# One inverse instead of two through DRAM, and memory attention in a written order, in a float32 two-block model

## The chip, the cores and the metric

The kernel runs on one core of a Trainium2 chip. What counts is the device time of one execution in microseconds (us). The engines of the core work side by side, each through its own list of instructions in order: TensorE (PE, with its weight loads as PEld), VectorE (DVE), ScalarE (ACT), GpSimd (POOL) and SyncE (SP), whose queue issues the loads of the weights. Semaphores tie the lists together. TensorE's clock has two levels, 1.2 and 2.4 GHz; the profile gives the granted clock as a share of the higher one.

## The reference

Two models stand one behind the other on one sequence of 256 tokens of width 1024, all in float32. The first has two layers of a mixer (three kinds of attention), a cross attention to 256 memory tokens, and an MLP, each with a layer norm behind it. The cross attention is:

```python
def memory_cross_attention(x, mem, w_q, w_kv, w_o):
    q = (x @ w_q).reshape(B, S, XA_HEADS, DH)                 # 4 heads of 64
    kv = (mem @ w_kv).reshape(B, M, 2, XA_HEADS, DH)
    k, v = kv[:, :, 0], kv[:, :, 1]
    s = jnp.einsum('bqhd,bmhd->bhqm', q, k) * (DH ** -0.5)
    p = jax.nn.softmax(s, axis=-1)
    o = jnp.einsum('bhqm,bmhd->bqhd', p, v).reshape(B, S, XA_W)
    return o @ w_o
x = layer_norm(DN_ALPHA * x + y, ln_g[l, 1], ln_b[l, 1])      # behind it
```

The second has two layers with three branches (a pooling mixer, retention, and an RWKV-7 recurrence), gated and merged. The recurrence goes token by token:

```python
def step(S, inp):
    r_t, w_t, k_t, v_t, a_t, b_t = inp
    sa = jnp.einsum('bhvk,bhk->bhv', S, a_t)
    S = S * w_t[:, :, None, :] + sa[..., None] * b_t[:, :, None, :] + v_t[..., None] * k_t[:, :, None, :]
    return S, jnp.einsum('bhvk,bhk->bhv', S, r_t)
```

## The kernel before

**Products.** Each float32 operand is split into a high part (`hi`, rounded) and the rest (`lo`), and a product is three matmuls, hi·hi, hi·lo and lo·hi (lines L138 to L140). Weights stream: SyncE's queue loads tiles of 512 KB into four buffers named `raw`, ScalarE casts `hi` (L112), VectorE, or GpSimd where a call says so, subtracts `lo` (L113); `hi` and `lo` have six buffers each. A matmul needs both, and a buffer `raw` comes free when its `lo` is done.

**Order.** A scheduler sets each engine's order from the order of the code and its own estimates of durations. Inside `tc.manual_schedule` TensorE's order is that of the code. PSUM banks are handed out by tag: four "mm", two "s", one "t", one "o". Copies out of PSUM by `evac` alternate between ScalarE (L283) and VectorE (L285).

**The recurrence in chunks.** Chunks of 64 tokens need the inverse of a triangular 64x64 matrix for each of eight heads and both halves of the partitions. The kernel writes the matrices to DRAM (`lt`), reads them back as 16x16 diagonal blocks, one to a partition, and inverts these by back substitution on VectorE (up to L1107) in `zrow`. It then copies `zrow` with rows and columns exchanged into `tb` (L1108), and GpSimd's queue writes both to scratch in DRAM: `td` from `tb` (L1111) and `zd` from `zrow` (L1112), each 128 KB. `inverse_parts` (L1116) reads them back as block diagonal tiles, `Tn` from `td` and `TT`, the transposed one, from `zd`, with eight reads of 128 KB (L1122). `invert` doubles the block size twice, with products of 64x64 matmuls (L1130), 16 instructions for one n of two. Meanwhile come retention's projections (`rv` evacuated by VectorE at L1322), its scores (L1334, L1339 on TensorE, masked by VectorE at L1336 and L1342), a gate (evacuated at L1292) and retention's outputs (L1351, L1354).

**How the recurrence is interleaved.** `recurrence` is a generator with 17 steps. `other_branches` is a second one with 16 yields, between which stand chunks of 12 matmuls of 512 columns or 24 of 256. In a `manual_schedule` the code takes one step of the one, then one of the other, and at last what is left of the others. At the recurrence's end VectorE normalises the outputs of each head (`ymu` L1250, `yvr` L1256, GpSimd's power at L174, L1258) and TensorE transposes them (`normed`, L1265).

**Memory attention** (block 1, once in each layer) lies between two norms. `us_k` and `us` are the weights of the keys and the query, split on GpSimd. `query` is 48 matmuls of 256 columns, `memory_values` 48, 24 for each half t of the tokens; `memory_scores` (L263) and the softmax (L266, L274), `memory_weights` (normalise L292, transpose L295), `attend_memory` (L307, with four casts and four subtractions of 128 columns), the output product with 12 matmuls of 512 columns for each t and c, and the second norm (`finish`: L338 and L340 on VectorE, transposes L343). Their order on TensorE is the scheduler's.

```python
        memory_keys(us_k)
        query(us)
        ps_ = [memory_scores(0)]
        memory_values()
        ps_.append(memory_scores(1))
```

Of the kernel before, what the change touches and what calls it, by code (L numbers as in the profile page):

```python
# [12 lines left out]
F32 = mybir.dt.float32  # L13
# [4 lines left out]
ALU = mybir.AluOpType  # L18
# [24 lines left out]
def program(ctx: ExitStack, tc: tile.TileContext, T: dict, out: bass.AP):  # L43
# [268 lines left out]
    class Norm:  # L312
# [17 lines left out]

        def finish(self, t):
            mv = st("mv", [128, 2])
            ver.bn_aggr(out=mv, in_=self.stats[t])
            r = rsqrt(mv[:, 1:2], LN_EPS)
            for i in range(2):
# [3 lines left out]
                                         op0=ALU.subtract, op1=ALU.mult)  # L339
                ver.scalar_tensor_tensor(out=z, in0=z, scalar=r, in1=self.b[:, s], op0=ALU.mult, op1=ALU.add)  # L340
                p = pst("s" if self.op else ("s", "s", "t", "o")[2 * t + i])
                for k in range(4):
# [37 lines left out]
    def block1_layer(l, x, xop, us, K):  # L380
# [352 lines left out]

        def memory_values():
            us = [unit(T["xa_kv"][l, 2 + i], 256, 4) for i in range(2)]
            o = [pst("mm"), pst("mm")]
            gemm_a(o, memop, us, n=256)
            for t in range(2):
                act.copy(out=xakv[:, 1, t], in_=o[t][:, :256])

# [6 lines left out]
        def memory_scores(t):  # L747
            return scores(256, lambda i: (xq[64 * (i // 2):64 * (i // 2) + 64, i % 2, tok(t)],
                                          xakv[64 * (i // 2):64 * (i // 2) + 64, 0, i % 2, :]), None)

        def memory_weights(P, sums):
            sc = st("sc", [128, 4])
            ver.reciprocal(out=sc, in_=sums)
            return transposed(P, sc, 256, ("s", "t"))

        def attend_memory(t, pt):
            for pr in range(2):
                pv_pair(xo, pr, t, lambda half: [(xakv[:, 1, kt, 128 * pr + 64 * half:128 * pr + 64 * half + 64],
                                                  pt[kt][:, pr + 2 * half, :]) for kt in range(2)])

# [17 lines left out]
        memory_keys(us_k)  # L778
        query(us)
        ps_ = [memory_scores(0)]  # L780
        memory_values()
        ps_.append(memory_scores(1))
        us = [unit(T["xa_o"][l, i], 512, 2) for i in range(2)]
        nrm2 = Norm(x)
        nrm2.params(l, 1)
        ahead = [unit(T["w_up"][l, i], 512, 2) for i in range(4)]
        ps_ = [memory_weights(*p) for p in ps_]
        for t in range(2):
            attend_memory(t, ps_[t])
            for c in range(2):  # L790
                o = [None, None]
                o[t] = pst("mm")
                gemm_a(o, xo, us[c:c + 1])
                nrm2.add(t, c, o[t])
            nrm2.finish(t)
        xop = nrm2.op
# [107 lines left out]
    def block2_layer(l, x, r, us, K, xop):  # L904
# [196 lines left out]
        for i in range(14, -1, -1):  # L1101
# [23 lines left out]
        def invert(Tn):  # L1125

# [142 lines left out]

        def recurrence(Tn):  # L1270

            yield from invert(Tn)
# [50 lines left out]

        Tn = inverse_parts()
        oop = Op([None, None, None])
# [231 lines left out]

    scratch = {n: dr.tile([128 * 2080], F32, name=n) for n in ("zd", "td", "lt")}

# [248 lines left out]
```

## Time and profile before

| | |
|---|---|
| median of 3 runs | 1672.89 us (1668.97 to 1673.03) |
| profiled execution, its own time | 1675.49 us |
| span in the trace | 1673.6 us |
| mean granted clock of TensorE | 0.973 |
| TensorE busy | 1588.1 us, 95% |
| VectorE, ScalarE, GpSimd busy | 1104.7, 742.7, 280.1 us |
| moved from and to HBM | 282.52 MB read, 6.88 MB written |

Block 1 ends at about 965 us of the span, block 2 fills the rest. A row of waits names the waiting engine and line, what released it, the sum in us, how often, and the longest. A row of a line of time gives start, duration, engine, line, operation, tiles and shape, and in brackets the idle time before and what ended it.

### The profile page before, as it was taken

Reading aid. Unit: us, or ns where it says so; the run is one execution under the profiler, and the core shown is the slowest. Engines: PE = TensorE matmul, PEld = TensorE weight load, DVE = VectorE, ACT = ScalarE, POOL = GpSimd, SP = SyncE. Lnnn points to the kernel's source line nnn. Section 1 sums busy time; section 2 is a strip of 40 time slices with the busy share of each in tenths; the row PEclk is TensorE's granted clock in tenths of the full one; section 3 lists DMA queues with packets and bytes.
Section 4 is the critical chain, followed back from the end, with each engine's and each line's share of the span. In section 5 each row is a group of like instructions: output and inputs, shape, how many; then the busy total and the mean of one; then the engine's idle time right before and its main releaser. Section 6 shows DMA issues by size and latency. Waiting matters only on the chain. (4 is left out here: it accounts for less than half of the span.)

```text
span 1673.6 us, 29627 instructions
## 1 busy us (share of the span) xinstructions
PE 1588.1 (95%) x11978; PEld 1442.6 (86%) x11978; DVE 1104.7 (66%) x1801; ACT 742.7 (44%) x1212; POOL 280.1 (17%) x266
## 2 busy tenths in 40 slices
PE   7999998999999999998999989889999999699998
PEld 6787997798878888986989879879999889699997
DVE  5557567876776665678966677665556677555654
ACT  4655444454445654444544364323443643233441
POOL 1000112111100000231201132401111313201202
PEclk9899999999999999999999979989999989899999
DMA  8732466487776333663777835643355345533552
GB/s 295 265 127 76 139 206 209 139 282 263 266 252 208 101 102 102 199 204 124 252 247 264 280 105 170 160 129 114 113 187 180 102 139 167 152 105 112 175 179 74
DMA packets 81752, 291.34 MB, mean 174 GB/s; under 512 B 9400, under 2 KB 10496, under 8 KB 81616
## 3 DMA queue, kind: packets, MB, share of 16 engines
q1 hardware_dynamic: 78768, 280.07, 50.8%
q0 software_dynamic: 2848, 9.39, 2.2%
q8 instruction: 94, 1.54, 0.4%
q14 instruction: 42, 0.34, 0.1%
HBM read 282.52 MB, written 6.88 MB: 173 GB/s over the span
## 5 line engine op out<-in xcount | busy, mean ns | idle before, releaser
L113 DVE TENSOR_TENSOR lo<-raw,hi 128x1024 fp32r<-128x1024 f32 (+1 forms) x421 | 532.8, 1272 | 282.1 <-ACT hi L112 280.5
L112 ACT CAST hi<-raw 128x1024 fp32r<-128x1024 f32 (+1 forms) x435 | 452.7, 1048 | 581.5 <-PE mm L139 242.6
L138 PE MATMUL mm<-act,hi 128*128 128x256 f32 x1808 | 523.3, 290 | 2.0 <-DVE act L130 2.0
L139 PE MATMUL mm<-act,hi 128*128 128x256 f32 x1808 | 520.0, 288 | 0.0
L140 PE MATMUL mm<-act,lo 128*128 128x256 f32 x1808 | 518.9, 287 | 0.0
L138 PEld LDWEIGHTS mm<-act,hi 128*128 128x128 f32 x1808 | 351.4, 194 | 7.2 <-issue 2.7
L139 PEld LDWEIGHTS mm<-act,hi 128*128 128x128 f32 x1808 | 351.0, 194 | 4.7 <-issue 4.3
L140 PEld LDWEIGHTS mm<-act,lo 128*128 128x128 f32 x1808 | 350.7, 194 | 2.6 <-issue 2.3
L138 PE MATMUL s<-act,hi 128*128 128x256 f32 x448 | 128.2, 286 | 6.9 <-ACT PT L834 4.3
L138 PE MATMUL mm<-hi,act 128*128 128x512 f32 (+1 forms) x320 | 125.1, 392 | 5.5 <-ACT hi L127 4.9
L140 PE MATMUL s<-act,lo 128*128 128x256 f32 x448 | 127.6, 285 | 0.0
L139 PE MATMUL s<-act,hi 128*128 128x256 f32 x448 | 127.6, 285 | 0.0
L139 PE MATMUL mm<-lo,act 128*128 128x512 f32 (+1 forms) x320 | 123.6, 386 | 0.8 <-DVE lo L113 0.8
L140 PE MATMUL mm<-hi,act 128*128 128x512 f32 (+1 forms) x320 | 123.2, 385 | 0.0
L138 PEld LDWEIGHTS s<-act,hi 128*128 128x128 f32 x448 | 86.8, 194 | 8.3 <-ACT PT L834 4.9
L139 PEld LDWEIGHTS s<-act,hi 128*128 128x128 f32 x448 | 86.7, 194 | 0.2
L140 PEld LDWEIGHTS s<-act,lo 128*128 128x128 f32 x448 | 86.8, 194 | 0.0
L839 POOL TENSOR_TENSOR PT<-PT 128x512 f32<-128x512 f32 x28 | 38.6, 1378 | 241.2 <-ACT P L838 115.1
L138 PEld LDWEIGHTS mm<-hi,act 128*128 128x128 f32 x320 | 60.9, 190 | 19.5 <-ACT hi L127 4.9
L1545 DVE CUSTOM_DVE_ANT_0 raw<-raw,gt 128x1024 f32<-128x1024 f32 x48 | 59.9, 1250 | 26.0 <-DMA raw<-in_w_ada 25.9
L138 PE MATMUL mm<-hi,P 128*128 128x512 f32 x192 | 74.8, 390 | 0.0
L139 PE MATMUL mm<-lo,P 128*128 128x512 f32 x192 | 74.8, 390 | 0.0
(486 smaller groups left out, 2418.2 us busy)
## 6 DMA issues: line engine op xcount, KB each, us to landing
raw<-in_w_in SPq DMA_DIRECT2D x119, 512.0 KB, 4.8
raw<-in_w_up SPq DMA_DIRECT2D x64, 512.0 KB, 4.7
raw<-in_w_down SPq DMA_DIRECT2D x64, 512.0 KB, 4.7
raw<-in_w_gate SPq DMA_DIRECT2D x48, 512.0 KB, 3.3
raw<-in_w_ada SPq DMA_DIRECT2D x48, 512.0 KB, 4.7
raw<-in_w_gl SPq DMA_DIRECT2D x48, 512.0 KB, 3.5
raw<-in_w_branch SPq DMA_DIRECT2D x24, 512.0 KB, 3.4
raw<-in_w_br SPq DMA_DIRECT2D x16, 512.0 KB, 3.3
```

The costliest lines, as they stand in the source:

```text
L112: act.copy(out=h[:, :cols], in_=r[:, :cols])
L113: (eng or ver).tensor_sub(out=l[:, :cols], in0=r[:, :cols], in1=h.bitcast(F32)[:, :cols])
L138: pe.matmul(o, lhsT=lh, rhs=rh, start=first, stop=False)
L139: pe.matmul(o, lhsT=lh, rhs=rl, start=False, stop=False)
L140: pe.matmul(o, lhsT=ll, rhs=rh, start=False, stop=last)
L839: pool.tensor_mul(out=r, in0=r, in1=r)
L1545: ver.tensor_tensor_reduce(out=r, in0=r, in1=box["c"], scale=1.0, scalar=0.0, op0=ALU.mult, op1=ALU.add, accum_out=mods[l][:, o:o + 1])
```

## The change

In block 2 the scratch `td`, its copy and its write are removed, and so are the reads of `Tn`. `Tn` is made in `invert` from `TT` by a product with the identity on TensorE, in a step of its own; `recurrence` has 18 steps with it. `zd` is written and `TT` is read as before. In block 1 the key and query weights of memory attention are split on VectorE; TensorE's order from the query to the first transposes of the second norm is written out; the scores of the second tokens take "mm" banks; the attention product of one t uses one bank, with one cast and one subtraction of 256 columns; `finish` of the norm is cut in `normalize` and `transpose`.

```diff
-        tb = bt("dg", [128, 16, 16])
-        ver.tensor_copy(out=tb, in_=bass.AP(tensor=zb.tensor, offset=zb.offset + 15,
-                                            ap=[list(zb.ap[0]), [16, 16], [15, 16]]))
-        pool.dma_start(out=flat(K["td"], 1, *blocks), in_=tb)
         pool.dma_start(out=flat(K["zd"], 16, *blocks), in_=zrow)
...
         def inverse_parts():
-            Tn = [bt("Tn", [128, 8, 64]) for n in range(2)]
             for n in range(2):
-                for d, t in ((K["td"], Tn[n]), (K["zd"], TT[n])):
-                    for a in range(2):
-                        pool.dma_start(out=t[half(a)], in_=flat(d, 16 + 8 * HS * n + 64 * 129 * a, [128, 64], [HS, 8], [1, 64]))
-            return Tn
+                for a in range(2):
+                    pool.dma_start(out=TT[n][half(a)], in_=flat(K["zd"], 16 + 8 * HS * n + 64 * 129 * a, [128, 64], [HS, 8], [1, 64]))
...
             of = lambda t: lambda i, a: t[half(a), i, :]
+            Tn = [bt("Tn", [128, 8, 64]) for n in range(2)]
+            for n in range(2):
+                p = pst("to"[n])
+                product(p, of(TT[n]), lambda i, a: ident[half(a), half(a)])
+                evac(flat2(Tn[n]), p)
+            yield
             for lv in range(2):
...
-            for _ in recurrence(Tn):
+            for _ in recurrence():
                 next(others, None)
...
-    scratch = {n: dr.tile([128 * 2080], F32, name=n) for n in ("zd", "td", "lt")}
+    scratch = {n: dr.tile([128 * 2080], F32, name=n) for n in ("zd", "lt")}
```

The memory attention after the change, from the same diff:

```diff
-        us_k = [unit(T["xa_kv"][l, i], 256, 4, pool) for i in range(2)]
-        us = [unit(T["xa_q"][l, i], 256, 4, pool) for i in range(2)]
+        us_k = [unit(T["xa_kv"][l, i], 256, 4) for i in range(2)]
+        us = [unit(T["xa_q"][l, i], 256, 4) for i in range(2)]
...
         def memory_scores(t):
+            ps_ = [pst("s" if t == 0 else "mm") for _ in range(2)]
+            for i in range(2):
+                for g, p in enumerate(ps_):
+                    pe.matmul(p[:, 256 * i:256 * i + 256], lhsT=xq[64 * g:64 * g + 64, i, tok(t)],
+                              rhs=xakv[64 * g:64 * g + 64, 0, i, :], start=True, stop=True)
+            return ps_
...
         def attend_memory(t, pt):
+            p = pst("ot"[t])
             for pr in range(2):
+                for kt in range(2):
+                    for half in range(2):
+                        pe.matmul(p[64 * half:64 * half + 64, 128 * pr:128 * pr + 128],
+                                  lhsT=xakv[:, 1, kt, 128 * pr + 64 * half:128 * pr + 64 * half + 64],
+                                  rhs=pt[kt][:, pr + 2 * half, :], start=kt == 0, stop=kt == 1)
+            h, lo = xo.parts[0]
+            split_op(h[:, :, tok(t)], lo[:, :, tok(t)], p[:, 0:256].rearrange("p (a b) -> p a b", b=128))
...
+        with tc.manual_schedule(engines={mybir.EngineType.PE}):
+            query(us)
+            ps_ = [memory_scores(t) for t in range(2)]
+            Ps = [memory_softmax(p) for p in ps_]
+            us_v = [unit(T["xa_kv"][l, 2 + i], 256, 4) for i in range(2)]
...
+            for t in range(2):
+                memory_values(t, us_v)
+                pts.append(memory_weights(t, Ps[t]))
+            for t in range(2):
+                attend_memory(t, pts[t])
...
+                nrm2.normalize(t)
+            nrm2.transpose(0)
+        nrm2.transpose(1)
```

GpSimd's order in the first layer of block 2, before, from the write of the inverses to the last read (`row` and `gt` are retention's rotary embedding, `zd` and `td` the scratch):

```order
L1112 DMA zd<-PT_10409 2048x1x16
L1111 DMA td<-dg_10443 2048x1x16
L1306 TENSOR_TENSOR row_10754<-row_10754,sin 128x256
L1122 DMA TT_10447<-zd 64x8x64
L1309 TENSOR_TENSOR gt_10643<-gt_10643,row_10754 128x256
L1306 TENSOR_TENSOR row_10760<-row_10760,sin 128x256
L1122 DMA Tn_10843<-td 64x8x64
L1309 TENSOR_TENSOR gt_10643<-gt_10643,row_10760 128x256
L1122 DMA Tn_10843<-td 64x8x64
L1122 DMA TT_10447<-zd 64x8x64
L1122 DMA Tn_10844<-td 64x8x64 x2
L1122 DMA TT_10448<-zd 64x8x64 x2
```

The same stretch of GpSimd after (its lines have moved by some 40):

```order
L1153 DMA zd<-PT_10401 2048x1x16
L1350 TENSOR_TENSOR row_10743<-row_10743,sin 128x256
L1161 DMA TT_10436<-zd 64x8x64
L1353 TENSOR_TENSOR gt_10632<-gt_10632,row_10743 128x256
L1350 TENSOR_TENSOR row_10749<-row_10749,sin 128x256
L1161 DMA TT_10436<-zd 64x8x64
L1353 TENSOR_TENSOR gt_10632<-gt_10632,row_10749 128x256
L1161 DMA TT_10437<-zd 64x8x64 x2
```

One write and four reads have left the queue, and nothing stands between the remaining reads but the rotary embedding.

VectorE's order at the recurrence's end in the same layer, before (`PT` holds the outputs, `ymu` and `yvr` their means and variances, `lo` a weight tile's rest):

```order
L1252 TENSOR_TENSOR PT_12049<-t_12023,ymu_12050 128x4x64
L1252 TENSOR_TENSOR PT_12049<-o_12024,ymu_12063 128x4x64
L113 TENSOR_TENSOR lo_12246<-raw_12243,hi_12245 128x1024
L1256 TENSOR_REDUCE yvr_12056<-dg_12054 128x4
L1256 TENSOR_REDUCE yvr_12069<-dg_12067 128x4
L172 TENSOR_SCALAR rs_12058<-yvr_12056 128x4
L172 TENSOR_SCALAR rs_12071<-yvr_12069 128x4
L113 TENSOR_TENSOR lo_12252<-raw_12249,hi_12251 128x1024
L1258 TENSOR_TENSOR PT_12049<-PT_12049,rs_12060 128x4x64
L1258 TENSOR_TENSOR PT_12049<-PT_12049,rs_12073 128x4x64
```

The same place after:

```order
L113 TENSOR_TENSOR lo_12267<-raw_12264,hi_12266 128x1024
L113 TENSOR_TENSOR lo_12273<-raw_12270,hi_12272 128x1024
L1294 TENSOR_REDUCE ymu_12095<-t_12068 128x4
L1294 TENSOR_REDUCE ymu_12108<-o_12069 128x4
L1295 TENSOR_SCALAR ymu_12095<-ymu_12095 128x4
L1295 TENSOR_SCALAR ymu_12108<-ymu_12108 128x4
L1296 TENSOR_TENSOR PT_12094<-t_12068,ymu_12095 128x4x64
L1296 TENSOR_TENSOR PT_12094<-o_12069,ymu_12108 128x4x64
L1300 TENSOR_REDUCE yvr_12101<-dg_12099 128x4
L1300 TENSOR_REDUCE yvr_12114<-dg_12112 128x4
L172 TENSOR_SCALAR rs_12103<-yvr_12101 128x4
L172 TENSOR_SCALAR rs_12116<-yvr_12114 128x4
```

The two weight splits stand ahead of the chain of the norm instead of inside it.

VectorE's order in the norm ahead of memory attention, before (`xr` are the rows of the residual stream, `gt` the norm's gain and bias):

```order
L328 SCALAR_TENSOR_TENSOR xr_1037<-xr_1037,mm_2650 128x512
L329 BN_STATS bn_2545<-xr_1037 128x6
L333 BN_AGGR mv_2738<-bn_2545 128x2
L172 TENSOR_SCALAR rs_2740<-mv_2738 128x1
L338 SCALAR_TENSOR_TENSOR xr_1037<-xr_1037,mv_2738,gt_2700 128x512 x2
L340 SCALAR_TENSOR_TENSOR xr_1037<-xr_1037,rs_2742,gt_2702 128x512 x2
L328 SCALAR_TENSOR_TENSOR xr_1039<-xr_1039,mm_2651 128x512
```

The same place after:

```order
L113 TENSOR_TENSOR lo_2720<-raw_2717,hi_2719 128x1024
L328 SCALAR_TENSOR_TENSOR xr_1036<-xr_1036,mm_2649 128x512
L329 BN_STATS bn_2544<-xr_1036 128x6
L337 BN_AGGR mv_2737<-bn_2544 128x2
L172 TENSOR_SCALAR rs_2739<-mv_2737 128x1
L342 SCALAR_TENSOR_TENSOR xr_1036<-xr_1036,mv_2737,gt_2699 128x512 x2
L113 TENSOR_TENSOR lo_2726<-raw_2723,hi_2725 128x1024
L113 TENSOR_TENSOR lo_2732<-raw_2729,hi_2731 128x1024
L344 SCALAR_TENSOR_TENSOR xr_1036<-xr_1036,rs_2741,gt_2701 128x512 x2
L328 SCALAR_TENSOR_TENSOR xr_1038<-xr_1038,mm_2650 128x512
```

Two splits now stand between the first pass of the norm and its second.

## Rows read from the trace of the kernel before

**Rows 1.** Table of busy time: engine, busy us, share of the span, instructions.

```profile
PE 1588.1 (95%) x11978; PEld 1442.6 (86%) x11978; DVE 1104.7 (66%) x1801; ACT 742.7 (44%) x1212; POOL 280.1 (17%) x266
```

**Rows 2.** TensorE's waits, whole run: us in total, times, longest us.

```profile
PE mm L1339 <- DVE kT L1292: 16.6, 2, 9.8
PE s L343 <- DVE xr L340: 7.0, 8, 2.1
...
PE mm L1334 <- DVE gt L1322: 4.7, 2, 2.9
PE mm L1351 <- DVE gt L1336: 4.4, 2, 3.3
...
PE t L1265 <- DVE PT L1258: 4.1, 2, 2.0
...
PE s L295 <- ACT P L274: 2.5, 2, 1.2
```

**Rows 3.** Windows: length; busy PE, PEld, DVE, ACT, POOL; clock, DMA, GB/s.

```profile
1070.00:1080.00 10.00, 10.00 (x86) 10.00 (x85) 2.79 (x3) 2.22 (x3) 3.03 (x5) 1.00 0.93 155
1080.00:1101.00 21.00, 8.27 (x48) 7.05 (x49) 12.40 (x21) 7.26 (x8) 4.57 (x7) 0.76 0.88 217
1428.00:1451.00 23.00, 10.00 (x51) 8.49 (x51) 12.90 (x21) 6.22 (x7) 6.61 (x9) 0.70 0.72 196
```

**Rows 4.** VectorE's line of time in the first stall stage.

```profile
1093.20 1.23 DVE L113 TENSOR_TENSOR lo<-raw,hi 128x1024 fp32r<-128x1024 f32 x1 [5.77 <-ACT hi L112]
1094.34 0.68 DVE L1292 SCALAR_TENSOR_TENSOR kT<-kT,mm 128x512 f32<-128x512 f32 x1
```

**Rows 5.** DMA issues of 1062 to 1100: size, median us to landing.

```profile
raw<-in_w_in SPq DMA_DIRECT2D x9, 512.0 KB, 9.0
...
TT<-zd POOLq DMA_DIRECT2D x4, 128.0 KB, 8.8
Tn<-td POOLq DMA_DIRECT2D x4, 128.0 KB, 6.4
zd<-PT POOLq DMA_DIRECT2D x1, 128.0 KB, 9.1
td<-dg POOLq DMA_DIRECT2D x1, 128.0 KB, 11.7
```

**Rows 6.** Queue 1 in 1070:1078, 1079:1081, 1082:1090: packets, MB, share of engines.

```profile
q1 hardware_dynamic: 227, 0.82, 77.5%
...
q1 hardware_dynamic: 205, 0.75, 95.3%
...
q1 hardware_dynamic: 186, 0.68, 39.4%
```

**Rows 7.** The chain that ended last, 1099 to 1107: start, us, what.

```profile
1100.95 1.08 PE t L1130 x32
1102.03 0.93 PE o L1130 x32
...
1103.39 0.23 PE mm L139
```

**Rows 8.** VectorE's line of time at the recurrence's end.

```profile
1193.64 1.23 DVE L113 TENSOR_TENSOR lo<-raw,hi 128x1024 fp32r<-128x1024 f32 x1 [0.97 <-ACT hi L112]
...
1199.15 0.43 DVE L1258 TENSOR_TENSOR PT<-PT,rs 128x256 f32<-128x256 f32 x1 [0.90 <-POOL rs L174]
```

**Rows 9.** Windows behind the recurrence's end, first and second layer.

```profile
1201.00:1204.60 3.60, 3.60 (x20) 3.60 (x19) 1.75 (x1) 2.82 (x6) 2.39 (x1) 0.53 0.02 5
1551.00:1554.50 3.50, 3.50 (x31) 3.50 (x30) 1.75 (x1) 3.15 (x6) 2.41 (x1) 1.00 0.00 0
```

**Rows 10.** VectorE's line of time in the norm ahead of memory attention.

```profile
259.52 5.63 DVE L340 SCALAR_TENSOR_TENSOR xr<-xr,rs,gt 128x512 f32<-128x512 f32 x2
...
269.21 1.41 DVE L340 SCALAR_TENSOR_TENSOR xr<-xr,rs,gt 128x512 f32<-128x512 f32 x2
```

**Rows 11.** Window behind that norm.

```profile
266.00:269.30 3.30, 3.30 (x17) 3.30 (x17) 3.27 (x8) 0.49 (x1) 0.94 (x1) 0.51 0.94 269
```

More of the change, by code (lines that the diff above doesn't have):

```diff
@@ L331, in finish, with normalize @@
         def finish(self, t):
+            self.normalize(t)
+            self.transpose(t)
+        def normalize(self, t):
             mv = st("mv", [128, 2])
@@ L340, in finish, with transpose @@
                 ver.scalar_tensor_tensor(out=z, in0=z, scalar=r, in1=self.b[:, s], op0=ALU.mult, op1=ALU.add)
+        def transpose(self, t):
+            for i in range(2):
+                z = self.x[t][:, 512 * i:512 * i + 512]
                 p = pst("s" if self.op else ("s", "s", "t", "o")[2 * t + i])
@@ L732, in memory_keys, with memory_values @@
             act.copy(out=flat2(xakv[:, 0]), in_=p)
-        def memory_values():
-            us = [unit(T["xa_kv"][l, 2 + i], 256, 4) for i in range(2)]
-            o = [pst("mm"), pst("mm")]
+        def memory_values(t, us):
+            o = [None, None]
+            o[t] = pst("mm")
             gemm_a(o, memop, us, n=256)
-            for t in range(2):
-                act.copy(out=xakv[:, 1, t], in_=o[t][:, :256])
+            act.copy(out=xakv[:, 1, t], in_=o[t][:, :256])
         def query(us):
@@ L747, in memory_scores @@
         def memory_scores(t):
-            return scores(256, lambda i: (xq[64 * (i // 2):64 * (i // 2) + 64, i % 2, tok(t)],
-                                          xakv[64 * (i // 2):64 * (i // 2) + 64, 0, i % 2, :]), None)
-        def memory_weights(P, sums):
+            ps_ = [pst("s" if t == 0 else "mm") for _ in range(2)]
+            for i in range(2):
+                for g, p in enumerate(ps_):
+                    pe.matmul(p[:, 256 * i:256 * i + 256], lhsT=xq[64 * g:64 * g + 64, i, tok(t)],
+                              rhs=xakv[64 * g:64 * g + 64, 0, i, :], start=True, stop=True)
@@ new lines, in memory_scores, with memory_softmax @@
+            return ps_
+        def memory_softmax(ps_):
+            P, sums, nmx = bt("P", [128, 4, 256], F32, 4), st("sums", [128, 4]), st("nmx", [128, 4])
+            for g, p in enumerate(ps_):
+                ver.tensor_reduce(out=nmx[:, 2 * g:2 * g + 2], in_=p.rearrange("p (h k) -> p h k", k=256), axis=AX.X,
+                                  op=ALU.max, negate=True)
+                for i in range(2):
+                    h = 2 * g + i
+                    act.activation(out=P[:, h, :], in_=p[:, 256 * i:256 * i + 256], func=AF.Exp,
+                                   bias=nmx[:, h:h + 1], accum_out=sums[:, h:h + 1])
@@ L752, in memory_weights @@
             sc = st("sc", [128, 4])
             ver.reciprocal(out=sc, in_=sums)
-            return transposed(P, sc, 256, ("s", "t"))
+            for kt in range(2):
+                Pk = P[:, :, 128 * kt:128 * kt + 128]
+                ver.tensor_mul(out=Pk, in0=Pk, in1=sc.unsqueeze(2).broadcast_to([128, 4, 128]))
+            return P
+        def memory_weights(t, P):
+            res = []
+            for kt in range(2):
+                p = pst(("s", "mm")[t])
+                for h in range(4):
+                    pe.transpose(p[:, 128 * h:128 * h + 128], P[:, h, 128 * kt:128 * kt + 128], ident)
+                res.append(bt("PT", [128, 4, 128], F32, 4))
+                evac(flat2(res[kt]), p)
+            return res
@@ L756, in attend_memory @@
         def attend_memory(t, pt):
+            p = pst("ot"[t])
             for pr in range(2):
-                pv_pair(xo, pr, t, lambda half: [(xakv[:, 1, kt, 128 * pr + 64 * half:128 * pr + 64 * half + 64],
-                                                  pt[kt][:, pr + 2 * half, :]) for kt in range(2)])
+                for kt in range(2):
+                    for half in range(2):
+                        pe.matmul(p[64 * half:64 * half + 64, 128 * pr:128 * pr + 128],
+                                  lhsT=xakv[:, 1, kt, 128 * pr + 64 * half:128 * pr + 64 * half + 64],
+                                  rhs=pt[kt][:, pr + 2 * half, :], start=kt == 0, stop=kt == 1)
@@ L778, in block1_layer @@
         memory_keys(us_k)
[L779 to L795, printed above, removed]
+        with tc.manual_schedule(engines={mybir.EngineType.PE}):
[3 more added lines that the diff above has]
+            us_v = [unit(T["xa_kv"][l, 2 + i], 256, 4) for i in range(2)]
+            us = [unit(T["xa_o"][l, i], 512, 2) for i in range(2)]
+            nrm2 = Norm(x)
+            nrm2.params(l, 1)
+            ahead = [unit(T["w_up"][l, i], 512, 2) for i in range(4)]
+            pts = []
+            for t in range(2):
[3 more added lines that the diff above has]
+                attend_memory(t, pts[t])
+                for c in range(2):
+                    o = [None, None]
+                    o[t] = pst("mm")
+                    gemm_a(o, xo, us[c:c + 1])
+                    nrm2.add(t, c, o[t])
+                nrm2.normalize(t)
+            nrm2.transpose(0)
+        nrm2.transpose(1)
         xop = nrm2.op
@@ L1116, in inverse_parts, with invert @@
         def inverse_parts():
-            Tn = [bt("Tn", [128, 8, 64]) for n in range(2)]
             for n in range(2):
-                for d, t in ((K["td"], Tn[n]), (K["zd"], TT[n])):
-                    for a in range(2):
-                        pool.dma_start(out=t[half(a)], in_=flat(d, 16 + 8 * HS * n + 64 * 129 * a, [128, 64], [HS, 8], [1, 64]))
-            return Tn
-        def invert(Tn):
+                for a in range(2):
+                    pool.dma_start(out=TT[n][half(a)], in_=flat(K["zd"], 16 + 8 * HS * n + 64 * 129 * a, [128, 64], [HS, 8], [1, 64]))
+        def invert():
             def product(p, lhs, rhs):
@@ L1268, in normed, with recurrence @@
                                scale=col(69, ct), bias=col(73, ct))
-        def recurrence(Tn):
-            yield from invert(Tn)
+        def recurrence():
+            yield from invert()
             S = st("S", [128, 4, 64], bufs=1)
@@ L1322, in block2_layer @@
             ver.tensor_copy(out=rv[:, t, :], in_=o[t])
-        Tn = inverse_parts()
+        inverse_parts()
         oop = Op([None, None, None])
```

## The prediction

> **What bounds the kernel now.** I read the table of busy time first. TensorE works 1588.1 of 1673.6 us, 95% [rows 1], so a change can save time only by taking matmuls away (this one takes none away, it adds some), by filling the 1673.6 − 1588.1 = 85.5 us in which TensorE stands, or by keeping the granted clock up. The second view says where it stands: TensorE's waits over the whole run [rows 2]. The three longest that come twice, once in each layer of the second block, are 16.6, 4.7 and 4.4 us, 25.7 us together, and all are for VectorE (lines L1292, L1322, L1336, the evacuations of retention's and the gates' products). The reader should ask why VectorE is late there, since it is busy 66% of the run only.
>
> The third view, windows, shows that these waits are one stage: in 1080 to 1101 us TensorE works 8.27 of 21 us, in 1428 to 1451 10.00 of 23, so 12.7 and 13.0 us are missing, while the DMA engines are 0.88 and 0.72 busy [rows 3]. The fourth view, VectorE's own line of time, gives the reason: `lo` of a weight tile starts at 1093.20 after 5.77 us of nothing, released by ScalarE's `hi`, and the evacuation L1292 for which TensorE stands comes right behind it [rows 4]. VectorE takes its instructions in order; the split stands ahead of the evacuation and waits for its weight tile. So the stage waits for weight loads, and VectorE is only the messenger.
>
> The fifth view, the DMA issues of 1062 to 1100, shows what is slow: nine weight tiles of 512 KB take 9.0 us each from issue to landing, and among them fly two writes of 128 KB (zd 9.1, td 11.7 us) and eight reads (TT 8.8, Tn 6.4 us) [rows 5]. While writes fly, queue 1, the weights, moves 0.82 MB in the 8 us from 1070 on, 0.103 MB/us; with nearly nothing beside it, 0.75 MB in 2 us, 0.375 MB/us; while the eight reads fly, 0.68 MB in 8 us, 0.085 MB/us [rows 6]. The share of the small transfers is small in bytes and large in time.
>
> **The change, part by part: transfers.** Per layer of block 2 one write (td) and four reads (Tn) go. Weights run at 0.103 of 0.375, 27%, while both writes fly, so 73% of the longer write's 11.7 us is lost to them: 8.5 us; I give half to td, 4.3. The reads cost 1 − 0.085/0.375 = 77% of 8 us, 6.2; four of the eight go, 3.1. So 7.4 us per layer come back to the loads, of the 12.7 and 13.0 that are missing, and since the stage waits for loads, TensorE gets them: −14.8 us. Half is a choice. Were the transfers worth their bytes alone, it would be (128 + 512 KB) at 0.375 MB/us, 1.7 per layer; were the whole stall due to the crowding, 25.7 in both. The value taken lies in the middle of these, and is what the queue's rates say.
>
> **Transposes on TensorE.** Instead of Tn's reads, two products with the identity, 32 instructions of 64x64 each. The trace has two such products one behind the other in the same function: 1.08 and 0.93 us in the chain that ended last [rows 7]. 2.01 us per layer, on the path since TensorE sets it: +4.0. Their evacuation (one copy on ScalarE, one on VectorE) stands behind a new step, and between it and the first use lie twelve matmuls of 512 columns at 0.23 us [rows 7], 2.8 us. The nearest row for such a copy is one 128x512 pass of 0.68 us [rows 4], so this is hidden; without cover it would cost about 0.7 per layer. The GpSimd instructions that go (the td issue and four reads) stood beside TensorE's work and are worth nothing of themselves. The clearing of td at the start runs beside a TensorE that doesn't stand: nothing.
>
> **The recurrence's end.** The recurrence has one step more now, and the other branches are still handed out one to a step, so each chunk of them lies one step earlier against it. At the end 24 matmuls of 256 columns fewer lie between the last products and the transposes that wait for the normed rows. 86 such matmuls filled 10 us [rows 3], 0.116 each, so 2.8 us of cover go. What the transposes wait for gets shorter too: before, two `lo` splits of 1.23 us stood between the links of that chain on VectorE (one starts at 1193.64, the last link at 1199.15) [rows 8]; in the new order both stand ahead of it. 2.8 − 2.5 = 0.3; with some waiting for `hi` ahead of it I take 0.5 per layer on top of the 4.1 in both layers that are waited there now [rows 2]: +1.0. Bounds 0 and 2.8 per layer.
>
> A longer wait there may also cost clock. Behind the first layer's 2 us wait the granted clock is 0.53 for 3.6 us, the lower level of 1.2 GHz; behind the same wait in the second it is 1.00 [rows 9]. At half clock 3.6 us do 1.8 us of work: some 1.7 per layer, not in the sum, in the range. [...]
>
> **Memory attention**, twice in block 1. The splits of its query and key weights go from GpSimd to VectorE, and TensorE's order is written out. Gain: two splits on GpSimd slow VectorE beside them, the pair L340 takes 5.63 us there and 1.41 alone [rows 10]. The new pair with two splits of 1.23 ahead is 3.9, so 1.8 earlier, and the transposes that wait for it (2.1 us at the longest [rows 2]) wait that much less. The granted clock falls to 0.51 right behind this wait [rows 11]: of 3.3 us half, 1.6, could come back. Loss: before, the softmax of the first tokens had 48 value matmuls to hide behind, now 24: at 0.116 us 2.8 us of cover less, where 1.2 were waited already [rows 2]. And the normed rows of the first tokens have 15 instead of 26 wide matmuls before their transposes: 11 at 0.23, 2.5. Joined banks take the pieces of 0.4 to 0.7 us away that the old order left between score, cast and product. Best: 1.8 + 1.6 + 1.2 = −4.6; worst: 2.8 + 2.5 − 1.8 = +3.5; I take −1.5, below the middle, since both losses count only as far as TensorE has nothing else ready: −3.0 in both layers.
>
> Sum against the profiled execution's 1675.49 us: −14.8 + 4.0 + 1.0 − 3.0 = −12.8, so 1662.7. That execution lies 2.6 above the median, so on the median of 1672.89 it is 1660.1; I say 1660.
>
> **The rivals.** D, better: the stall is a knot and not a queue. Once loads come in time, nothing waits, all of 25.7 goes, and with it the clock of 0.76 and 0.70 in those windows [rows 3], 2 to 3 us more. −25.7 − 2.5 + 4.0 + 1.0 − 4 (memory a little better) = −27, so 1646. For it: VectorE and ScalarE are far from full. Against: half of the small transfers stay, and weights still come at the rate of the queue.
>
> B, no change: the removed transfers are worth their bytes only. What holds queue 1 is then how its own tiles' buffers come free, and the slow rate a sign of that. 1.7 per layer: −3.4 + 4.0 + 1.0 − 3.0 = −1.4, 1671.5. Against it: the rate falls to 0.103 MB/us with DMA engines 0.93 busy [rows 3, 6], which isn't a queue with nothing to do. The Trainium skill ("DMA: Bandwidth & Descriptors", section "Why small descriptors are slow (HBM only)") puts the price of small pieces at a fixed overhead, 11 cycles for 8 with 256 bytes, and so 5 for 2 with 64. By it, as an estimate, the four reads cost 512 KB × 1.38 and the write 128 KB × 2.5 at that rate, 2.8 per layer, and the sum would be −3.6, 1669.3. The rates of [rows 6] speak for more than this.
>
> C, slower: the stall stays and the price is paid. The one write and four reads that are left fly at the same place and still hold the loads of the stage, so it gives nothing; the identity products then only add, 4.0, and their extra step leaves the recurrence's end bare, 2.8 per layer with none of it made up by the splits: 4.0 + 5.6 − 3.0 = +6.6, 1679.5. It decides where the stage gives back under 0.8 us per layer. For it: VectorE waits for a single tile, and one late tile is enough. Against: the td write alone takes 11.7 us.
>
> **How the numbers follow.** The forecast has 0.57, with a range of its own from 1653 (memory at its best) to 1667 (the tail bare, or 4 us per layer from the stage). D 0.15, B 0.15, C 0.13. A measurement of this kernel can't tell less than 0.3%, 5 us, from no change: 1667.9 to 1677.9. Faster is forecast and D, less a sliver: 0.71; same B and the sliver: 0.16; slower C: 0.13. The range reaches from D's 1646 and a little below to the upper side of B: 1644 to 1675.
>
> **What would show it.** In the profile after: windows of the two stall stages with TensorE idle some 5 us instead of 13; weight tiles landing in under 9.0 us there; two identity products of about 2 us on the path; the transposes at the recurrence's end waiting 2 to 3 us; the pair L340 no longer at 5.6 us. The forecast is wrong if the waits for L1292, L1322 and L1336 together stay above 20 us, or if memory attention shows new waits of more than 4 us per layer for its softmax or its norm.

## The result and the profile after

The changed kernel takes 1653.94 us (median of nine runs, 1650.95 to 1663.39) against 1672.89 of before in the same nine rounds (1668.97 to 1682.66). The ratio is 0.9895, its 95% interval 0.9869 to 0.9920: 13 to 22 us less, 17.6 at the middle. Forecast were 1660 and −12.8. The profiled execution shown here took 1650.95 us, 24.5 less than the one of before; it is the fastest of the nine, so its stages are compared one by one and not as a sum.

The table of busy time after; it answers to [rows 1]:

```profile
PE 1582.1 (96%) x12106; PEld 1441.1 (87%) x12106; DVE 1109.2 (67%) x1805; ACT 743.7 (45%) x1210; POOL 250.0 (15%) x247
```

TensorE's waits over the whole run (us in total, times, longest); they answer to [rows 2]:

```profile
PE mm L1383 <- DVE kT L1336: 9.5, 2, 5.1
...
PE s L858 <- ACT PT L879: 4.9, 2, 2.8
PE t L1309 <- DVE PT L1302: 3.9, 2, 1.9
PE s L784 <- DVE P L776: 3.3, 2, 1.8
...
PE s L351 <- DVE xr L344: 1.1, 2, 0.8
...
PE mm L1395 <- DVE gt L1380: 0.5, 1, 0.5
```

The lines have moved: L1383 was L1339, L1395 was L1351, L1309 was L1265, L351 was L343. The stall of block 2 was 16.6 + 4.7 + 4.4 = 25.7 us and is 9.5 + 0.5 = 10.0; the wait for L1334 is gone. The recurrence's end waits as before. L784 and L858 are new or longer.

Windows of the stall stages of both layers and of the time behind the recurrence's end (columns as in [rows 3]):

```profile
1070.00:1091.00 21.00, 15.99 (x183) 13.75 (x181) 14.76 (x38) 6.78 (x8) 2.05 (x2) 0.84 0.54 181
1410.00:1433.00 23.00, 17.86 (x195) 15.20 (x195) 17.93 (x42) 6.35 (x8) 3.24 (x4) 0.85 0.55 173
...
1189.00:1192.60 3.60, 3.60 (x33) 3.60 (x32) 1.44 (x1) 3.56 (x7) 2.33 (x1) 1.00 0.00 0
1530.00:1533.60 3.60, 3.60 (x32) 3.60 (x31) 3.56 (x5) 1.26 (x2) 0.00 (x0) 1.00 0.43 146
```

TensorE stands 5.0 and 5.1 us where it stood 12.7 and 13.0, and the DMA engines are 0.54 and 0.55 busy where they were 0.88 and 0.72.

The DMA issues of 1045 to 1090 (size, median us to landing); they answer to [rows 5]:

```profile
raw<-in_w_in SPq DMA_DIRECT2D x11, 512.0 KB, 4.2
...
TT<-zd POOLq DMA_DIRECT2D x4, 128.0 KB, 4.2
zd<-PT POOLq DMA_DIRECT2D x1, 128.0 KB, 7.9
```

A weight tile lands in 4.2 us instead of 9.0, and the reads that stayed in 4.2 instead of 8.8; the write that stayed is hardly faster (7.9, was 9.1). The weights' queue in 1056:1064, while that one write flies, and in 1064:1072, while the four reads do; this answers to [rows 6]:

```profile
q1 hardware_dynamic: 219, 0.82, 67.2%
...
q1 hardware_dynamic: 444, 1.63, 57.8%
```

Beside one write the weights move no faster than they did beside two, 0.82 MB in 8 us; the two flew for 12.8 us (1066.10 to 1078.9), the one for 7.9. As an estimate from these rows, a packet of the weights holds an engine for 0.39 us beside the one write (67.2% of 16 engines' 8 us for 219 packets), 0.44 beside two, and 0.15 when nearly alone. So the second write did not slow the loads further, it kept them slow for longer. Beside four reads the weights move 1.63 MB in 8 us, beside eight it was 0.68.

VectorE's line of time there, with the end of the recurrence further down; it answers to [rows 4, 8]:

```profile
1074.42 1.22 DVE L113 TENSOR_TENSOR lo<-raw,hi 128x1024 fp32r<-128x1024 f32 x1 [2.14 <-ACT hi L112]
1075.56 0.68 DVE L1336 SCALAR_TENSOR_TENSOR kT<-kT,mm 128x512 f32<-128x512 f32 x1
...
1087.39 0.67 DVE L285 COPY Tn<-o 128x512 f32<-128x512 f32 x1
...
1178.78 1.22 DVE L113 TENSOR_TENSOR lo<-raw,hi 128x1024 fp32r<-128x1024 f32 x1 [0.21 <-ACT hi L112]
...
1187.45 0.42 DVE L1302 TENSOR_TENSOR PT<-PT,rs 128x256 f32<-128x256 f32 x1 [0.90 <-POOL rs L174]
```

What is left of the stall is the same knot, smaller: a `lo` that waits for its tile, and the evacuation L1336 right behind it.

TensorE's line of time at the identity products, 32 instructions for each n (the 16 named for such a product count the calls in the code); it answers to [rows 7]:

```profile
1083.94 1.21 PE L1168 MATMUL t<-cpack,TT 64*64 64x64 f32 x32
1084.99 1.10 PE L1168 MATMUL o<-cpack,TT 64*64 64x64 f32 x32
1086.02 0.50 PE L138 MATMUL mm<-hi,act 128*128 128x512 f32 x1
...
1088.96 1.15 PE L1168 MATMUL t<-Tn,LT 64*64 64x64 f32 x32
```

From 1083.94 to 1086.02 the products take 2.08 us. The later of their two copies, on VectorE, ends at 1088.06, 0.9 us before the first use: hidden.

### The profile page after: what moved, and what is told of

Same layout as the page of the kernel before. It is cut to its first block, busy times and chain, and to the rows that moved or that the text cites. A ratio compares the mean times of both kernels' runs of the same rounds, so it can differ in the third digit from the quotient of the medians.

```text
span 1648.8 us, 29886 instructions
## 1 busy us (share of the span) xinstructions
PE 1582.1 (96%) x12106; PEld 1441.1 (87%) x12106; DVE 1109.2 (67%) x1805; ACT 743.7 (45%) x1210; POOL 250.0 (15%) x247
## 4 chain that ended last, share of the span: by engine, by line
PE 38%; DVE 7%; DMA 3%; issue 2%; ACT 2%; POOL 1%; DVEq 0%; POOLq 0%; ACTq 0%
PE mm L138 9%; PE mm L139 9%; PE mm L140 8%; DVE lo L113 2%; DMA raw<-in_w_in 2%; PE s L138 2%; PE s L139 2%; PE s L140 2%; ACT hi L112 1%; DMA dg<-lt 1%; PE s L1120 1%; PE o L1236 1%; DVE dg L1151 1%; DMA lt<-P 1%; PE t L1236 1%
## 5 line engine op out<-in xcount | busy, mean ns | idle before, releaser
L113 DVE TENSOR_TENSOR lo<-raw,hi 128x1024 fp32r<-128x1024 f32 (+1 forms) x429 | 543.6, 1273 | 278.4 <-ACT hi L112 274.3
L140 PE MATMUL mm<-act,lo 128*128 128x256 f32 x1808 | 515.4, 286 | 0.0
L138 PEld LDWEIGHTS mm<-act,hi 128*128 128x128 f32 x1808 | 347.8, 192 | 6.7 <-DVE act L130 2.4
L139 PEld LDWEIGHTS mm<-act,hi 128*128 128x128 f32 x1808 | 347.6, 192 | 5.4 <-issue 4.0
L140 PEld LDWEIGHTS mm<-act,lo 128*128 128x128 f32 x1808 | 347.2, 192 | 2.9 <-issue 2.0
L140 PE MATMUL s<-act,lo 128*128 128x256 f32 x448 | 127.9, 285 | 0.0
L140 PE MATMUL mm<-hi,act 128*128 128x512 f32 (+1 forms) x320 | 122.9, 384 | 3.0 <-DVE act L128 3.0
L140 PEld LDWEIGHTS s<-act,lo 128*128 128x128 f32 x448 | 87.1, 194 | 0.0
L138 PEld LDWEIGHTS mm<-hi,act 128*128 128x128 f32 x320 | 60.8, 190 | 19.9 <-ACT hi L127 5.3
L140 PEld LDWEIGHTS mm<-hi,act 128*128 128x128 f32 x320 | 61.0, 191 | 15.8 <-DVE act L128 4.3
```

Of the source, the lines that this page charges most:

```text
L113: (eng or ver).tensor_sub(out=l[:, :cols], in0=r[:, :cols], in1=h.bitcast(F32)[:, :cols])
L138: pe.matmul(o, lhsT=lh, rhs=rh, start=first, stop=False)
L139: pe.matmul(o, lhsT=lh, rhs=rl, start=False, stop=False)
L140: pe.matmul(o, lhsT=ll, rhs=rh, start=False, stop=last)
```

## The experiments

Each ratio is to the kernel before, on the chip and in the rounds of the run. "Stall" is the sum of TensorE's waits in the stall stages of both layers, from its three lines (L1334, L1339, L1351 and their counterparts), in the one profiled execution of each kernel. The medians come from several chips, on which the kernel before stands at 1669 to 1673 us, so kernels are compared by their ratios.

| run | median us | ratio (95%) | stall us |
|---|---|---|---|
| before | 1672.89 | 1 | 25.7 |
| after | 1653.94 | 0.9895 (0.9869 to 0.9920) | 10.0 |
| inverses alone | 1656.45 | 0.9922 (0.9899 to 0.9945) | 10.8 |
| memory attention alone | 1663.47 | 0.9961 (0.9944 to 0.9978) | 22.9 |
| after, small pieces back | 1670.60 | 0.9999 (0.9983 to 1.0015) | 26.0 |
| after, same bytes in large pieces | 1662.07 | 0.9950 (0.9929 to 0.9970) | 17.3 |
| after, write back | 1664.97 | 0.9977 (0.9961 to 0.9993) | 19.1 |
| after, reads back | 1657.53 | 0.9935 (0.9911 to 0.9960) | 10.4 |
| after, clearing back | 1654.61 | 0.9920 (0.9902 to 0.9938) | 11.2 |
| after, values first | 1653.84 | 0.9916 (0.9894 to 0.9939) | 10.1 |
| after, splits on GpSimd | 1657.62 | 0.9911 (0.9885 to 0.9937) | 9.9 |
| before, splits on VectorE | 1668.92 | 0.9981 (0.9964 to 0.9998) | 23.1 |
| after, compact write | 1648.98 | 0.9855 (0.9833 to 0.9877) | 7.3 |
| after, compact write, pads | 1650.71 | 0.9873 (0.9850 to 0.9895) | 7.1 |

How far the stall differs between executions shows in kernels whose block 2 has the same transfers: 22.9 to 26.0 us with all of them (before, memory attention alone, splits on VectorE, small pieces back), 9.9 to 11.2 without (after, inverses alone, values first, splits on GpSimd, clearing back). A difference of a microsecond or two is therefore no finding.

**The two halves of the change.** Each was put alone into the kernel before.

> The kernel before with the change of the inverses alone; memory attention as before. My theory (small pieces hold the weight queue, memory attention gives little): the idle time of TensorE in the two stall stages falls from 12.7 and 13.0 us to about 5 each, the identity products add 2.0 us per layer, so about 1661 to 1663 us against 1673, a ratio of 0.993 to 0.995. Rival, that most of the gain comes from memory attention: 1669 or more, ratio over 0.997, and stall stages that lose less than 5 us each.

> The kernel before with the change of memory attention alone; the inverses as before. My theory: the pair L340 in the norm ahead is no longer stretched (3.9 instead of 5.6 us) and TensorE's wait of 2.1 us there goes, a new wait of 1.5 us for the softmax comes, and the sum is -2 to -6 us, 1667 to 1671, ratio 0.996 to 0.999; stall stages in block 2 unchanged at 12 to 13 us each. Rival, that most of the gain is here: 1658 to 1662, ratio 0.990 to 0.993.

The inverses alone give −13.0 us (−16.9 to −9.2), memory attention alone −6.5 (−9.4 to −3.7); together −19.5, and the whole change −17.6. They add up, and two thirds are the inverses. The stall follows the inverses (10.8) and not memory attention (22.9). The rival that memory attention is the gain has fallen.

**Are the small pieces the cause?** The removed transfers were put back into the changed kernel as dead load; the products stayed.

```diff
+        tb = bt("dg", [128, 16, 16])
+        ver.tensor_copy(out=tb, in_=bass.AP(tensor=zb.tensor, offset=zb.offset + 15,
+                                            ap=[list(zb.ap[0]), [16, 16], [15, 16]]))
+        pool.dma_start(out=flat(K["td"], 1, *blocks), in_=tb)
         pool.dma_start(out=flat(K["zd"], 16, *blocks), in_=zrow)
...
+                    pool.dma_start(out=Tn[n][half(a)], in_=flat(K["td"], 16 + 8 * HS * n + 64 * 129 * a, [128, 64], [HS, 8], [1, 64]))
                     pool.dma_start(out=TT[n][half(a)], in_=flat(K["zd"], 16 + 8 * HS * n + 64 * 129 * a, [128, 64], [HS, 8], [1, 64]))
...
-    scratch = {n: dr.tile([128 * 2080], F32, name=n) for n in ("zd", "lt")}
+    scratch = {n: dr.tile([128 * 2080], F32, name=n) for n in ("zd", "td", "lt")}
```

> The changed kernel with the removed transfers put back as dead load: the copy tb, the write of td in pieces of 64 B and the four reads of 256 B pieces into the tiles Tn, which the identity products then overwrite; nothing else changes. My theory (the pieces hold the weights' queue): the stall stages come back to 11 to 13 us of TensorE idle each, the time rises by 12 to 16 us on the changed kernel's 1654, to 1666 to 1670. Rival, that they are worth their bytes (640 KB per layer): 1.7 us per layer, 1657. Rival, that the stages shrank because the order moved with the products: no change, 1654.

TensorE's waits from 1060 to 1450 in that run:

```profile
PE mm L1388 <- DVE kT L1341: 15.4, 2, 8.8
PE mm L1400 <- DVE gt L1385: 5.4, 3, 2.7
PE mm L1383 <- DVE gt L1371: 5.2, 2, 3.2
```

26.0 us: the stall is back in full, line by line as in [rows 2], and the time is that of the kernel before. So the transfers are the cause (with the copy `tb` and the clearing of `td` that came back beside them), and not the new order that came with the products. Then the same bytes in large pieces:

```diff
-        pool.dma_start(out=flat(K["td"], 1, *blocks), in_=tb)
+        pool.dma_start(out=flat(K["td"], 0, [256, 128], [16, 16], [1, 16]), in_=tb)
...
-                    pool.dma_start(out=Tn[n][half(a)], in_=flat(K["td"], 16 + 8 * HS * n + 64 * 129 * a, [128, 64], [HS, 8], [1, 64]))
+                    pool.dma_start(out=Tn[n][half(a)], in_=flat(K["td"], 0, [512, 64], [64, 8], [1, 64]))
```

> As the run with the small pieces back, with the same bytes in the same instructions at the same places, but in large pieces: the write in 128 pieces of 1 KB, the reads in 64 pieces of 2 KB (all four read the same 128 KB). My theory, that number and size of the pieces matter: less than half of the loss of the run with small pieces, 1656 to 1660, stall stages at 5 to 8 us. Rival, that bytes or the mere presence of five transfers more matter: the same time as the run with small pieces.

```profile
PE mm L1388 <- DVE kT L1341: 10.2, 2, 6.2
PE mm L1400 <- DVE gt L1385: 6.0, 3, 3.1
PE mm L1383 <- DVE gt L1371: 1.1, 1, 1.1
```

17.3 us of stall, 7.3 over the changed kernel where small pieces gave 16.0. The size of the pieces makes 8.7 of the 16; the other 7.3 come without it, twice the 3.4 that the bytes would take by the rate in [rows 6]. What makes them, the bytes or five more instructions in GpSimd's order, these runs don't separate. Neither side of this expectation held alone: 1662 lies above my 1656 to 1660 and below the rival's 1670.

**Write or reads?** The run with small pieces, cut in two.

> The changed kernel with the copy tb and the write of td (2048 pieces of 64 B) back as dead load, and td cleared at the start; no reads. The prediction gave the write 4.3 us per layer. By it the stall stages go from 5.1 to some 9 us of TensorE idle each and the time to 1662 to 1664. Rival, that the reads do it: stages below 6.5 us, 1654 to 1658. Rival, that the stage is filled by any one of the two (a knot): 12 us each already here, 1668 to 1670.

> The changed kernel with the four reads of td (512 pieces of 256 B each) back as dead load into Tn, and td cleared at the start; no write. The prediction gave the reads 3.1 us per layer: stages at some 8 us each, 1660 to 1662. Rival, that the write does it all: stages below 6.5 us, 1654 to 1658.

TensorE's waits from 1060 to 1450, first with the write back:

```profile
PE mm L1387 <- DVE kT L1340: 8.6, 2, 5.0
PE mm L1382 <- DVE gt L1370: 7.4, 2, 4.0
PE mm L1399 <- DVE gt L1384: 3.1, 2, 1.6
```

and with the reads back, with the time of these reads below (shortest, median and longest issue in ns, then first and last start in us):

```profile
PE mm L1384 <- DVE kT L1337: 7.5, 2, 3.8
PE mm L1396 <- DVE gt L1381: 2.9, 2, 2.2
...
L1162 POOL DMA_DIRECT2D Tn<-td x8: 687/698/755, 771.9 to 1114.0; - x8
```

The write alone adds 9.1 us of stall (7.9 against the run below that has only the clearing back), 4.5 per layer where 4.3 were priced. The run with the reads does not price them: with no write to wait for, GpSimd's queue issues the four of the first layer at 771.93 to 775.94 us and the four of the second at 1108.77 to 1113.96, far from the stall stages (about 1070 to 1100 and 1400 to 1450), so that its 10.4 us says nothing about reads inside them. Behind the write, where they wait for it to land and so fall into the stage, the same reads add 6.9 (26.0 − 19.1), 3.4 per layer, where 3.1 were priced. What reads would cost in the stage without that write was not tried.

**The clearing at the start.** It was thought free. Windows of 70 to 80 us in the changed kernel:

```profile
70.00:75.00 5.00, 4.95 (x25) 3.51 (x24) 2.06 (x6) 4.78 (x12) 0.21 (x1) 1.00 0.78 302
75.00:80.00 5.00, 5.00 (x26) 3.03 (x24) 2.89 (x10) 4.07 (x13) 1.05 (x2) 1.00 0.01 2
```

> The changed kernel with nothing put back but the clearing of td at the start (640 pieces of 1664 B, 1.06 MB, at about 43 us of the span). The prediction held it for free, since TensorE does not stand at 43 us. A new theory from the profiles of the runs so far: it delays weight loads until 70 to 75 us, where all kernels with td in the scratch wait 0.7 to 1.3 us (and lose up to 2 us more at the lower clock) and those without wait nothing: +1 to +3 us, 1655 to 1657. The prediction's view: no wait at 70 to 75 us and 1654.

The same windows with only the clearing of td back:

```profile
70.00:75.00 5.00, 3.71 (x18) 2.59 (x16) 3.02 (x5) 4.80 (x12) 0.00 (x0) 1.00 1.00 384
75.00:80.00 5.00, 4.96 (x19) 3.55 (x19) 1.63 (x10) 4.83 (x15) 0.20 (x1) 0.66 0.13 53
```

The profile shows what the new theory says: 1.3 us of TensorE idle and a granted clock of 0.66 behind it, as in the kernel before, with DMA at 1.00. That is 1.2 us and, at 0.66 for 5 us, up to 1.7 more. All eight kernels that clear `td` stand for 0.7 to 1.6 us between 60 and 80 us, the six that don't for less than 0.1; in the run with the reads back the wait comes at 60 to 70 us. The clock falls in some of the eight only. The time can't confirm it: the run with the values first, in the same rounds and without the clear, has 0.9916, and the intervals of 0.9920 and 0.9895 overlap too.

**Memory attention's parts.**

> The kernel before with only these splits moved to VectorE; order, banks and inverses as before. If the splits are the gain: 5 to 8 us less than before, as much or more than the whole memory part alone (ratio 0.995 to 0.997), since the new order's wait of 1.5 us for the softmax isn't paid. Rival: within 2 us of before, ratio 0.999 to 1.001.

> The changed kernel with the splits of the key and query weights of memory attention back on GpSimd; the written order and the joined banks stay. If the splits are the gain of the memory part (as I priced it, 1.8 us of the pair L340 and up to 1.6 of the clock per layer): the pair is stretched to 5 us again, TensorE waits 2 us there, and the time goes to 1657 to 1660. Rival, that the written order and the banks are the gain: no more than 1 us lost, 1654 to 1655.

TensorE's waits from 255 to 330 us (norm, memory attention, start of the MLP, first layer), some of their longest rows. Before, all rows together 7.6 us:

```profile
PE s L343 <- DVE xr L340: 3.0, 3, 2.1
PE s L138 <- DVE P L128: 1.5, 1, 1.5
PE s L295 <- ACT P L274: 1.2, 1, 1.2
```

Before with the splits on VectorE, 5.1 us; the wait for L340 has nearly gone:

```profile
PE s L343 <- DVE xr L340: 0.5, 2, 0.3
```

After, 7.0 us:

```profile
PE s L858 <- ACT PT L879: 2.1, 1, 2.1
PE s L784 <- DVE P L776: 1.5, 1, 1.5
PE mm L140 <- DVE act L128: 1.5, 1, 1.5
```

After with the splits on GpSimd, 10.4 us:

```profile
PE s L858 <- ACT PT L879: 3.1, 1, 3.1
PE s L351 <- DVE xr L344: 2.7, 2, 2.1
```

and there the pair is stretched again, on VectorE's line of time:

```profile
255.97 5.63 DVE L344 SCALAR_TENSOR_TENSOR xr<-xr,rs,gt 128x512 f32<-128x512 f32 x2
...
265.67 1.41 DVE L344 SCALAR_TENSOR_TENSOR xr<-xr,rs,gt 128x512 f32<-128x512 f32 x2
```

The splits take 2.5 us of wait away in the old order (7.6 to 5.1) and 3.4 in the new (10.4 to 7.0); the written order adds 2.8 with the splits on GpSimd and 1.9 with them on VectorE, through its waits for the softmax (L784), for the norm's second half (L140 for `act`) and in the MLP's first transposes (L858). In the second layer (725 to 800 us) the four sums are 8.1, 6.5, 8.3 and 10.1 us, the same signs. In the times the splits alone stand at −3.2 us (−6.0 to −0.3), short of the 5 to 8 expected, and the other two comparisons (memory alone against splits alone, after against splits on GpSimd) lie within their intervals. So by the waits the splits are the gain and the order gives part of it back; by the times this is not settled.

**The new wait for the softmax.** The values were put back ahead of the transposes:

```diff
             for t in range(2):
                 memory_values(t, us_v)
+            for t in range(2):
                 pts.append(memory_weights(t, Ps[t]))
```

> The changed kernel with one thing moved in the written order of memory attention: both halves of the values (48 matmuls) come before the first transposes of the softmax, as many as in the order before the change; nothing else. My theory, that the new wait of 1.5 to 1.8 us there is cover taken away: the wait goes, and with 0.5 us for the banks 1 to 1.5 us per layer are gained, 2 to 3 in all, 1651 to 1652; no new wait in its place over 0.5 us. Rival, that the softmax chain is held by the weights' splits ahead of it on VectorE and ScalarE, which move along: the wait stays over 1 us and the time stays at 1654.

TensorE's waits from 735 to 790 us, second layer, in this run:

```profile
PE o L794 <- DVE PT L285: 1.1, 1, 1.1
...
PE o L794 <- ACT PT L283: 0.7, 1, 0.7
PE mm L784 <- DVE P L776: 0.7, 1, 0.7
```

In the changed kernel L784 waits 1.8 us in this stretch and L794 0.2. Now L784 waits 0.7 and L794, the attention product, 1.8: the same time at the next step of the chain; that this is because the values that hid the second evacuation have moved too is my reading, not shown. There is no gain in the time (1653.84): my theory fell, and of the rival the time came true, but not the place of the wait.

**A version meant to beat both.** If the scattered write is what holds the weights, the one that is left should be turned round as well. The reads then also move 128 KB instead of 512 KB (16 of 8 KB, they were 4 of 128 KB), and `zd` is no longer cleared at the start, so the write isn't the only thing that changes.

```diff
-        pool.dma_start(out=flat(K["zd"], 16, *blocks), in_=zrow)
+        pool.dma_start(out=flat(K["zd"], 0, [272, 128], [1, 272]), in_=zrow.rearrange("p a b -> p (a b)"))
...
-                    pool.dma_start(out=TT[n][half(a)], in_=flat(K["zd"], 16 + 8 * HS * n + 64 * 129 * a, [128, 64], [HS, 8], [1, 64]))
+                    for q in range(4):
+                        pool.dma_start(out=TT[n][64 * a + 16 * q:64 * a + 16 * q + 16, :, 16 * q:16 * q + 16],
+                                       in_=flat(K["zd"], 272 * (64 * n + 4 * a + q), [16, 16], [8 * 272, 8], [1, 16]))
```

> The changed kernel with the remaining transfers turned around: zrow has rows of 17 and is written in 128 pieces of 1088 B instead of 2048 of 64 B, and the spreading is left to the reads, 16 of 128 pieces of 64 B instead of 4 of 512 pieces of 256 B, into tiles TT that GpSimd has set to zero; the scratch zd needs no clearing. Theory that came out of the runs so far (the scattered write to DRAM holds the weights' queue, scattered reads hardly): the stall stages fall from 5.1 us of TensorE idle to 1 to 3 each, 4 to 8 us in all, 1646 to 1650. Rival (pieces of 64 B cost alike on either side): stages stay at 4 to 6 us, 1653 to 1655. Rival (16 issues of 0.7 us on GpSimd make TT late): TensorE waits for TT at the first identity product, over 1657.

Its DMA issues of 1045 to 1100, and the weights' queue in 1056:1064, while its reads fly:

```profile
TT<-zd POOLq DMA_DIRECT2D x16, 8.0 KB, 3.9
zd<-PT POOLq DMA_DIRECT2D x1, 136.0 KB, 2.1
...
q1 hardware_dynamic: 541, 1.99, 76.7%
```

The write lands in 2.1 us instead of 7.9, and beside the reads the weights move 1.99 MB in 8 us, where they moved 0.82 beside the scattered write and 1.63 beside the four reads of the changed kernel. TensorE has no wait for TT, and the stall falls to 7.3 us. At 1648.98 us it is 21 to 28 us faster than before. Against the changed kernel, 0.9855 / 0.9895 is 0.4% less, with the two intervals' half widths (0.0022 and 0.0026) put together 0.34%; but the run below, the same kernel with a smaller clear, stands at only 0.22% less. That it beats the changed kernel isn't settled by the times. Of the 6.6 us between 0.9855 and 0.9895 the stall explains 2.7, less than the 4 to 8 expected; the rest isn't accounted for.

> The same, and of the scratch lt only the 16 pads of 512 B are cleared at the start that no write covers, instead of 1.06 MB; so nothing large is cleared any more. If the clears delay the weight loads before 75 us: 0 to 2 us less than the run with the compact write alone (TensorE has no wait left at 70 to 75 us in the changed kernel, so little is left to gain). It is the candidate for a version faster than both.

1650.71 us: no difference from the run above that can be measured.

## Why the prediction was right, step by step

- **The bound and its cause: right.** TensorE waited for VectorE, VectorE for a weight tile, and the tile for the queue beside the small transfers; putting these back brought all of it back. 14.8 us were forecast from the queue's rates in [rows 6], 25.7 − 10.0 = 15.7 were measured, 12 to 16 by the spread between executions.
- **How the 14.8 was divided: right as far as the runs tell, half of it by choice.** The write had 4.3 per layer and has 4.5. The reads had 3.1 and have 3.4 behind the write; alone they were never in the stage. Half of the longer write's time was given to `td` as a choice; the rows of the changed kernel bear it out, since one write holds the queue at the same 0.82 MB in 8 us as two, and the pair flew 12.8 us where one flies 7.9.
- **Identity products: right.** 4.0 forecast, 2.08 in the first layer measured; their copies are hidden as named.
- **The recurrence's end: mis-sized.** +1.0 was forecast; the waits are 3.9 where they were 4.1. VectorE's chain from the first `ymu` to the last link took 8.5 us (1191.05 to 1199.58) and takes 5.5 (1182.33 to 1187.87), so the splits that left it (the last now at 1178.78) paid for all of the lost cover. The clock behind is 1.00 in both layers, where it was 0.53 in one. So of four waits of 1.9 to 2.0 us at this place one was followed by the lower clock.
- **Memory attention: right in sign, its size not settled.** −3.0 was forecast, −6.5 (−9.4 to −3.7) measured for that half alone. Its gain is the pair L340 and the clock behind it (0.59 in 266 to 270 us and 0.50 in 735 to 740, now 1.00 in both), its loss the softmax and the norm, as named. But the waits of both layers together are 15.7 us before and 15.3 after, so they don't show the 6.5. The mean granted clock of that kernel's twelve runs is 0.9752 against 0.9736 for before, worth 2.6 us on TensorE's 1588 as an estimate; the rest isn't accounted for. The −1.5 per layer was picked between −4.6 and +3.5, and that the sign came right owes something to luck.
- **The clearing of `td`: the step that failed, by the profiles.** "The clearing of td at the start runs beside a TensorE that doesn't stand: nothing" looked at the time of the clear, 43 us. It was 1.06 MB beside DMA engines that were nearly full (0.83 busy in 60 to 70 us, 0.97 in 70 to 75). Weight tiles issued in 38 to 75 us land in 6.1 us with the clear back and in 5.5 in the changed kernel, and TensorE stands 30 us after the clear, mostly at 70 to 75 us; which load it misses was not traced. Worth 1 to 3 us by the profiles.
- **The sum: the result lies at the edge of the forecast's own range** (1653 to 1667). Of the 4.8 us between −12.8 and −17.6, the waits give 1.2 to the recurrence's end (+1.0 forecast, −0.2 measured) and 0.9 to the stall, the profiles 1 to 3 to the clear; what memory attention gave beyond its −3.0 can't be told from these.
- **Rivals.** B, bytes only, has fallen: the five transfers cost 8.0 us per layer (26.0 − 10.0 in both) and not 1.7. The overhead per piece that the Trainium skill gives ("DMA: Bandwidth & Descriptors", section "Why small descriptors are slow (HBM only)") made 2.8 of it by the estimate in the prediction; the stall puts it far higher, and nearly half of the cost (7.3 of 16.0) remains with pieces of 1 and 2 KB. C has fallen, since the stage gave back 7.8 us per layer. D has half a point: the stall went further in the compact version, to 7.3, but not to nothing.

## What to carry to other kernels

Price a small scattered transfer by how far the rate of the main queue falls while it flies, and look for the victim downstream: it may be an evacuation behind a split, or a load 30 us later. Here a write of 64-byte pieces held the weights most; written in long runs, with scattered reads of a quarter of the bytes, it held them least. When a transfer is put back as dead load, look in the trace where it flew before its cost is read off. And when cover is moved to hide one link of a chain, look at which link it hid before.

## What the runs showed of the hardware

A write of 128 KB to DRAM took 7.9 us in 2048 pieces of 64 B, and one of 136 KB in 128 pieces of 1088 B took 2.1 us at the same place; 16 reads of 128 pieces of 64 B, issued one behind the other, landed in 3.9 us each. Beside the scattered write the weights' queue moved 0.82 MB in 8 us, beside two such writes the same, beside the 16 reads 1.99 in their first 8 us. Two splits on GpSimd made a pair of VectorE passes of 1.41 us take 5.63, in each kernel that had them side by side.
